# Output gate of the recurrence with features on partitions, and it and the first branch gate by seven products

## The chip, the cores and the metric

The kernel runs on one core of a Trainium2 chip. The metric is the device time of one execution in microseconds (us). The engines are named as in the profile: PE is TensorE, the matrix engine (PEld its loads of the stationary operand), DVE is VectorE, ACT is ScalarE, POOL is GpSimd and SP is SyncE, which here only starts DMA loads. Each of them works through its own queue in order, and a semaphore wait at the head of a queue holds up all that stands behind it.

## The reference, cut to what matters

Two layers of a decoder trunk over 512 tokens of width 1024, in float32. Each layer has a feed-forward block, a mixer and a second feed-forward block. The change is in the mixer:

```python
h = rms_norm(x, gn[2])
proj = h @ w_in[l]
hq, hf, hi, hg, aq, ak, av, gate_a, gate_b = jnp.split(proj, IN_SPLITS, axis=-1)
y_hg = hgrn2_mixer(hq, hf, hi, hg, lb_all[l], hgrn_head_gain[l]) @ w_branch_hgrn[l]
y_at = swa_sink_attention(aq, ak, av, attn_sinks[l]) @ w_branch_attn[l]
mixed = jax.nn.sigmoid(gate_a) * y_hg + jax.nn.sigmoid(gate_b) * y_at
x = x + rms_norm(mixed @ w_out[l], gn[3])
# the end of hgrn2_mixer: o [tokens, 4 heads, 128] is the output of the recurrence
o = o * rsqrt(mean(o * o, axis=-1) + EPS) * head_gain
o = o.reshape(B, S, 512) * silu(g_out)          # g_out is hg
```

`hq, hf, hi, hg` are 512 wide (four heads of 128), the two branch gates 1024.

## The kernel before, in words

**Products.** Every float32 product is made of rounded parts: an operand is split into a high part (`whi`, or `s`) and the low rest (`wlo`), and `mm3` issues three matmuls per 128x128 block of the stationary operand: high by high, high by low, low by high. `project` makes 128 features on partitions by 512 tokens (8 blocks deep, 24 matmuls of 512 columns); `project_tok` makes four tiles of 128 tokens on partitions by 512 features (96 matmuls of 512 columns). `sevenths` makes two such sets of 128 features at once by seven products over half of the tokens and half of the depth each, as in Strassen's scheme: 84 matmuls of 256 columns and one `lead` of 144 columns, where two `project` take 48 of 512. It needs sums of the weights' quarters (made on DVE while the weights stream in, lines 340 to 345, from two tiles `w32` into `tt`) and sums of the operand's quarters, kept in `x56` and `x37`, and on DVE five steps that put the products together in `m` (L1063 to L1070).

**The stream of weights.** `ws` loads weights by SP (L247) into four tiles `w32`, and prepares at most a few units ahead. A unit is split on ACT (L359, cast of the high part), and its low part is made either by a subtraction on DVE (L363) or, for the kind "v", by a negated copy on ACT (L355) and an accumulating DMA of POOL (L358).

**Order.** PE's order is written by hand: it is the order of the program. The small matmuls of attention and of the recurrence are placed between the large products by `Order`: each of these jobs is a coroutine that yields a waiting time from the table `WAIT`, and goes on when the products issued since then add up to it by a fixed rate per column. The queues of DVE and ACT are set by a scheduler, and their order is part of the built program.

**The mixer before.** `quad` makes q and forget gates of heads 0 and 1 of the recurrence; then come the projections of attention (`kS`, `qS`, `vT`), the values `vs` (`project_tok`), the output gate `gs` (`project_tok`, token tiles on partitions, tanh on ACT at L1428, two steps on DVE at L1429 and L1431, the second with the head gain `hgh`), and the projections of heads 2 and 3. `head` applies the sigmoids (L1272 to L1274 on ACT, L1275 to L1277 on DVE). `recurrence_scores` and `chunk_states` run the recurrence in levels (on DVE L1172, L1177, L1188, and predicated copies at L1164). `outputs` makes a head's output: the matmuls into `aux`, a square on ACT (L1289), the mean and its root (L1291 to L1293), the normed output (L1295), four products with `gs` (L1300), four transposes and a split. `attend` makes one block of attention: scores, bias (L1357), maxima (L1362), eight exponentials on ACT (L1374), their sums and shares on DVE (L1378 to L1382), transposes, copies on ACT (L1396), the values' product. Then follow the first branch, eight times `branch` (one `project` for the gate, 12 matmuls for the branch itself), with the operand sums `pre.sums()` ahead of the last four, and the second branch, four times `branches`, whose gates come by `sevenths`. `aux` and `acc` are the PSUM banks, `big` is a pool of 61 tiles of 128x512 (named `s` in the profile).

**The gain rows.** `hgh`, the head gain on every partition, is loaded among the constants at the start; `gain_rows` halves it on DVE and makes the lower bounds `lb`, `oml` behind that.

Of the kernel before, what the change touches and what calls it, by code (L numbers as in the profile page):

```python
# [7 lines left out]
F32 = mybir.dt.float32  # L8
F32R = mybir.dt.float32r
# [24 lines left out]
    head=2600.0, level=5000.0, last=3400.0, chunks=2600.0, states=2600.0, norm=2370.0, gate=8000.0,  # L34
    values=1200.0, scores=2000.0, exp=9000.0, shares=6000.0, turn=1900.0, turned=3000.0, rest=1200.0, lent=4200.0, apart=4000.0, block=2000.0, pair=4000.0, att0=1260.0, att1=12300.0,
)
W32, WS, AHEAD, TAIL, FIRST, EARLY, LATE = 4, 6, 3, 4, 7, 4, 8
# [9 lines left out]
def trunk(ctx: ExitStack, tc: tile.TileContext, xin, wall, gains, lbT, hgain, sinks, c_dist, c_mask, c_ident, out):  # L47
# [111 lines left out]
    class Stream:  # L159
# [29 lines left out]
        def gates(self):  # L189


            u, v, h = self.n, self.wall, (slice(0, D // 2), slice(D // 2, D))
            self.src[u + 1] = [(h[0], wall[v + 1][:, h[1]]), (h[1], wall[v + 2][:, h[0]])]
            self.src[u + 2] = [(h[0], wall[v + 1][:, h[0]]), (h[1], wall[v + 2][:, h[1]])]
            self.pairs(1)
            self.plain(1)
# [41 lines left out]
        def load(self, upto):  # L238
            while self.dma < min(upto, self.n):
                w = sb.tile([P, D], F32, tag="w32", name=nm("w32"), bufs=W32)  # L240
                u = self.dma
                if isinstance(self.src[u], list):
                    for c, a in self.src[u]:
                        nc.sync.dma_start(w.rearrange("p (m c) -> p m c", m=4) if c is None else w[:, c], a)  # L244
# [334 lines left out]
    class Pre(Quarters):  # L579


        def __init__(self, l, n):
# [5 lines left out]
            self.x56, self.x37 = [], []  # L588

        def sums(self):  # L590
# [6 lines left out]
            for x, v in zip((self.x56, self.x37), quarter_sums(a[0][0], a[1][0], a[0][1], a[1][1])):  # L597
                x.append(pair_split(v))

# [436 lines left out]
    def sevenths(pre, between=lambda: None, first=True):  # L1036
# [8 lines left out]
        p1, p26, p57, p43 = acc()[:, :H2], acc(), acc(), aux()  # L1045
# [220 lines left out]
    def mixer(l, pre, nxt):  # L1266
        vs, gs = [], []
# [12 lines left out]
        def outputs(i, h):  # L1280
# [15 lines left out]
            yield WAIT["norm"]  # L1296
            while len(gs) < TT:
                yield 500.0
            for t in range(TT):
                nc.vector.tensor_tensor(o[:, t, :], o[:, t, :], gs[t][:, i * P : (i + 1) * P], op=ALU.mult)  # L1300
            yield WAIT["gate"]
# [3 lines left out]
            oa[i] = split(pt)  # L1305
# [120 lines left out]
        for p in project_tok(pre):  # L1426
            g = big()
            nc.scalar.activation(out=g, in_=p, func=AF.Tanh, scale=0.5)  # L1428
            nc.vector.scalar_tensor_tensor(g, g, 1.0, p, op0=ALU.add, op1=ALU.mult)  # L1429
            gv = g.rearrange("p (i d) -> p i d", i=H)  # L1430
# [221 lines left out]
```

## Time and profile before

| | us |
|---|---|
| median of 3 runs (lowest, highest) | 2024.97 (2024.91, 2026.1) |
| the profiled execution | 2024.79 |
| its span in the trace | 2023.0 |
| PE busy | 2016.2 |
| DVE busy | 1624.3 |
| ACT busy | 1265.2 |
| POOL busy | 268.3 |

The mixer of layer 0 lies at about 338 to 650 us, that of layer 1 some 1000 us later. Rows of the timeline give start, duration, engine, line, operation, output and input, count, and in brackets the idle time before and what ended it. Rows of the chain give start, duration, engine, tile, line and count. Neighbouring steps of one engine overlap in the trace by a little, so what a step costs is read from start to start.

### The profile page before, as it was taken

How to read it: one execution, taken by the hardware profiler on the slowest of the kernel's cores; microseconds unless marked ns; L12 is line 12 of the kernel's file. 1: busy time of each engine (PE TensorE's matmuls, PEld its weight loads, DVE VectorE, ACT ScalarE, POOL GpSimd, SP SyncE). 2: the span in 40 equal slices, each digit the busy share in tenths (PEclk: the TensorE clock that was granted, in tenths of full speed). 3: DMA queues.
4: the chain of work that ended last, by engine and by line, in shares of the span. 5: the costliest groups of instructions: out<-in, count | busy, mean ns of one | idle time of the engine just before them, and what ended most of it. 6: DMA issues, size and time to landing. Idle time of an engine off the chain costs nothing.

```text
span 2023.0 us, 36425 instructions
## 1 busy us (share of the span) xinstructions
PE 2016.2 (100%) x13553; PEld 1809.1 (89%) x13553; DVE 1624.3 (80%) x2894; ACT 1265.2 (63%) x2213; POOL 268.3 (13%) x318
## 2 busy tenths in 40 slices
PE   9999999999999999999999999999999999999998
PEld 8899988877898999998899998898778989999987
DVE  5888899767786788888998888977686858888888
ACT  7566687447364566658766666864554646666684
POOL 0111140000000011113211111400000100111140
PEclk9999999999999999999999999999999999999999
DMA  8688798311246368879768888872122554788794
GB/s 257 159 193 198 177 203 244 109 63 64 83 104 208 112 158 190 193 189 208 202 170 196 196 190 203 189 223 86 61 74 63 151 182 123 170 193 200 175 202 122
DMA packets 166801, 328.07 MB, mean 162 GB/s; under 512 B 19072, under 2 KB 85088, under 8 KB 166624
## 3 DMA queue, kind: packets, MB, share of 16 engines
q1 hardware_dynamic: 122416, 228.16, 34.1%
q0 software_dynamic: 44064, 97.54, 28.5%
q8 instruction: 106, 1.74, 0.3%
q14 instruction: 71, 0.58, 0.1%
q10 hardware_dynamic: 144, 0.05, 0.0%
HBM read 213.43 MB, written 14.73 MB: 113 GB/s over the span
## 4 chain that ended last, share of the span: by engine, by line
PE 93%; DVE 3%; ACT 1%; DMA 1%; issue 1%; SPq 0%; DVEq 0%; ACTq 0%
PE acc L116 71%; PE aux L116 20%; PE aux L126 2%; DVE wlo L296 1%; DVE s L264 1%; DMA w<-wall 1%; PE acc L126 0%; ACT whi L288 0%; DVE s L968 0%; SPq L244 0%; ACT s L442 0%; ACT s L443 0%; DVE wlo L363 0%; DVE s L863 0%; DVE s L433 0%
## 5 line engine op out<-in xcount | busy, mean ns | idle before, releaser
L116 PE MATMUL acc<-s,whi 128*128 128x256 f32 (+1 forms) x4998 | 1018.9, 303 | 0.0
L116 PEld LDWEIGHTS acc<-s,whi 128*128 128x128 f32 x4998 | 791.5, 188 | 46.6 <-issue 3.2
L116 PE MATMUL acc<-s,wlo 128*128 128x256 f32 (+1 forms) x2488 | 752.5, 302 | 0.1
L116 PEld LDWEIGHTS acc<-s,wlo 128*128 128x128 f32 x2488 | 467.9, 188 | 23.3 <-DVE wlo L363 0.4
L116 PE MATMUL acc<-whi,s 128*128 128x512 f32 x1360 | 441.5, 393 | 0.0
L359 ACT CAST whi<-w 128x1024 fp32r<-128x1024 f32 (+1 forms) x310 | 286.1, 926 | 195.0 <-PE acc L116 124.5
L358 POOL DMA_DIRECT2D wlo<-w x178 | 154.6, 869 | 1200.2 <-ACT wlo L355 715.0
L116 PEld LDWEIGHTS acc<-whi,s 128*128 128x128 f32 x1360 | 255.3, 188 | 57.1 <-issue 3.2
L116 PE MATMUL acc<-wlo,s 128*128 128x512 f32 x680 | 265.5, 390 | 0.2 <-DVE wlo L296 0.2
L355 ACT ACTIVATE wlo<-w 128x1024 fp32r<-128x1024 f32 (+1 forms) x178 | 154.6, 869 | 137.1 <-PE aux L116 98.2
L116 PE MATMUL aux<-s,whi 128*128 128x256 f32 (+1 forms) x1296 | 226.9, 278 | 0.0
L359 ACT CAST whi<-tt 128x1024 fp32r<-128x1024 f32 x160 | 168.4, 1053 | 83.2 <-DVE tt L341 43.0
L363 DVE TENSOR_TENSOR wlo<-w,whi 128x1024 fp32r<-128x1024 f32 (+1 forms) x132 | 157.4, 1205 | 78.3 <-ACT whi L359 78.1
L363 DVE TENSOR_TENSOR wlo<-tt,whi 128x1024 fp32r<-128x1024 f32 x160 | 195.4, 1221 | 9.9 <-ACT whi L359 7.3
L116 PEld LDWEIGHTS aux<-s,whi 128*128 128x128 f32 x1296 | 195.8, 188 | 1.1 <-issue 0.5
L116 PE MATMUL aux<-s,wlo 128*128 128x256 f32 (+1 forms) x648 | 179.8, 277 | 0.0
L116 PEld LDWEIGHTS acc<-wlo,s 128*128 128x128 f32 x680 | 127.8, 188 | 27.0 <-DVE wlo L296 2.1
L116 PE MATMUL aux<-whi,s 128*128 128x512 f32 x432 | 143.7, 390 | 0.0
L444 POOL DMA_DIRECT2D s<-s x128 | 111.1, 967 | 223.5 <-ACT s L432 104.7
L116 PEld LDWEIGHTS aux<-s,wlo 128*128 128x128 f32 x648 | 121.6, 188 | 0.4
L296 DVE TENSOR_TENSOR wlo<-s,whi 128x512 fp32r<-128x512 f32 x160 | 102.7, 686 | 9.9 <-ACT whi L288 9.9
L1070 DVE TENSOR_TENSOR m<-aux,s 128x512 f32<-128x512 f32 x80 | 55.2, 690 | 52.0 <-PE aux L116 51.5
(184 smaller groups left out, 2485.1 us busy)
## 6 DMA issues: line engine op xcount, KB each, us to landing
w<-wall SPq DMA_DIRECT2D x267, 512.0 KB, 3.9
wlo<-w POOLq DMA_DIRECT2D x98, 512.0 KB, 5.4
w<-wall SPq DMA_DIRECT2D x224, 128.0 KB, 3.5
wlo<-w POOLq DMA_DIRECT2D x80, 256.0 KB, 4.2
s<-wall SPq DMA_DIRECT2D x128, 128.0 KB, 4.2
s<-s POOLq DMA_DIRECT2D x64, 256.0 KB, 4.6
x_d<-s SPq DMA_DIRECT2D x48, 256.0 KB, 4.7
s<-x_d SPq DMA_DIRECT2D x48, 256.0 KB, 5.1
```

What stands on the lines that cost most here:

```text
L116: nc.tensor.matmul(o, lhsT, rhs, start=start, stop=stop)
L126: nc.tensor.transpose(o, src, ident)
L264: pin(nc.vector.tensor_tensor(o[c], x[c], y[c], op=op))
L296: pin(nc.vector.tensor_tensor(it.lo[:, h[c]], w[c], it.hi[:, h[c]].bitcast(F32), op=ALU.subtract))
L355: i = nc.scalar.mul(it.lo[:, c], w[:, c], -1.0)
L358: nc.gpsimd.dma_start(it.lo[:, c].bitcast(F32), w[:, c], accum_op=ALU.add)
L359: i = nc.scalar.copy(it.hi[:, c], w[:, c])
L363: self.hold(nc.vector.tensor_tensor(it.lo[:, c], w[:, c], it.hi[:, c].bitcast(F32), op=ALU.subtract))
L444: nc.gpsimd.dma_start(lo.bitcast(F32), src, accum_op=ALU.add)
L1070: ws.hold(nc.vector.tensor_tensor(m[:, 1:3, :], pairs[2], v[:, ::-1, :], op=ALU.add))
```

## The change

The output gate `hg` is made with features on partitions, by two `sevenths`; tanh and product stand in `hg[i]`, and `outputs` transposes first and multiplies with the gain column `hcol` and `hg[i]` in one step on DVE that reads the transposes from PSUM. The eight plain gates of the first branch become four pairs by `sevenths`, with `acc` for its last bank. The operand sums are made earlier: `within` makes one of four after each of the four projections of heads 2 and 3, with the splits on ACT and by DMA of POOL, and `third` makes the operand of product 3 in place of the second half of `h` in the first gate product. Heads 2 and 3 are projected ahead of the gate. The gate's weights are loaded in four turned pieces each (`turned`), the branch's weights become kind "v". The head gain is loaded in `gain_rows`, into a tile of the pool, and brought on partitions by a product with the identity and a sum. New lines are 1 to 39 higher than old ones.

```diff
-W32, WS, AHEAD, TAIL, FIRST, EARLY, LATE = 4, 6, 3, 4, 7, 4, 8
+W32, WS, AHEAD, TAIL, FIRST, EARLY = 4, 6, 3, 4, 7, 4
+PLAIN = (False, False, False, False)
...
-        def gates(self):
+        def turned(self, v, n):
+
+            for m in range(0, n, 2):
+                for i in range(2):
+                    c = slice((m + i) * P, (m + i + 1) * P)
+                    self.src[self.n + i] = [
+                        (slice(2 * q * P, 2 * (q + 1) * P), wall[v + q].rearrange("p (i c) -> p i c", i=2)[:, :, c]) for q in range(KT // 2)
+                    ]
+                self.pairs(1)
+                self.wall -= 2
+
...
+        def sums(self):
+            for x, v in zip((self.x56, self.x37), self.quarters()):
                 x.append(pair_split(v))
+
+        def within(self):
+
+            s, t = self.quarters()
+            self.x56.append(pair_split(s, split_dma))
+            x = big(F32R, [P, 2, S // 2])
+            self.x7.append(split_dma(t[:, 1, :], to=(x[:, 0, :], x[:, 1, :])))
+            self.t3.append(t[:, 0, :])
+
+        def third(self):
+            while self.t3:
+                self.x3.append(split(self.t3.pop(0), to=cut(self.h[len(self.x3)], HALF[1])))
+
+        def operand(self, n):
+            if n in (3, 7) and self.x7:
+                return self.x3 if n == 3 else self.x7
+            return super().operand(n)
...
-    def sevenths(pre, between=lambda: None, first=True):
+    def sevenths(pre, between=lambda: None, first=True, get=aux):
...
-            yield WAIT["norm"]
-            while len(gs) < TT:
-                yield 500.0
-            for t in range(TT):
-                nc.vector.tensor_tensor(o[:, t, :], o[:, t, :], gs[t][:, i * P : (i + 1) * P], op=ALU.mult)
-            yield WAIT["gate"]
+            yield WAIT["outs"]
+            if hg[i] is None:
+                while hg[i] is None:
+                    yield 500.0
+                yield WAIT["norm"]
             pt = aux()
             for t in range(TT):
                 transpose(pt[:, t * P : (t + 1) * P], o[:, t, :])
-            oa[i] = split(pt)
+            g = hg[i]
+            nc.vector.scalar_tensor_tensor(g, pt, hcol[:, l, i % 2 : i % 2 + 1], g, op0=ALU.mult, op1=ALU.mult)
+            oa[i] = split(g)
...
-        for p in project_tok(pre):
-            g = big()
-            nc.scalar.activation(out=g, in_=p, func=AF.Tanh, scale=0.5)
-            nc.vector.scalar_tensor_tensor(g, g, 1.0, p, op0=ALU.add, op1=ALU.mult)
-            gv = g.rearrange("p (i d) -> p i d", i=H)
-            nc.vector.tensor_tensor(gv, gv, hgh[:, l : l + 1, :].to_broadcast([P, H, P]), op=ALU.mult)
-            gs.append(g)
-        order.spawn(run(2, [head(project(pre), project(pre), i) for i in range(2, H)]))
+        heads = []
+        for i in range(2, H):
+            pj = []
+            for _ in range(2):
+                pj.append(project(pre))
+                pre.within()
+            heads.append(head(*pj, i))
+        order.spawn(run(2, heads))
+
+        for i in range(0, H, 2):
+            v = sevenths(pre, lambda: pre.third(), get=acc)
+            for n in range(2):
+                g = big()
+                u = v[:, 2 * n : 2 * n + 2, :].rearrange("p i t -> p (i t)")
+                nc.scalar.activation(out=g, in_=u, func=AF.Tanh, scale=-0.5 if n else 0.5)
+                nc.vector.scalar_tensor_tensor(g, g, 1.0, u, op0=ALU.add, op1=ALU.mult)
+                hg[i + n] = g
...
-        def branches(get):
-
-            v = sevenths(pre)
+        def branches(get, bank=aux):
+
+            v = sevenths(pre, get=bank)
             src = get()
             for i in range(2):
...
-        for m in range(LATE):
-            if m >= LATE - 4:
-                pre.sums()
-            part.append(branch(attended))
-        part += [g for m in range(LATE, KT, 2) for g in branches(attended)]
+        for plain in PLAIN:
+            if plain:
+                part += [branch(attended) for _ in range(2)]
+            else:
+                part += list(branches(attended, acc))
...
-                ws.plain(2 * H + 2 + 8 + LATE * 3 // 2)
-                for _ in range(KT - LATE // 2):
+                ws.plain(10)
+                g = ws.wall
+                ws.wall += 4
+                ws.plain(4, "v")
+                ws.turned(g, H)
+                for plain in PLAIN:
+                    ws.gates(not plain)
+                for _ in range(KT // 2):
                     ws.gates()
                 ws.rows(KT, False)
...
-        pin(nc.vector.tensor_scalar(hgh, hgh, 0.5, None, op0=ALU.mult))
-
+        t = big(F32, [P, DEPTH, 2, P])
+        nc.sync.dma_start(t[:, :, 0, :], hgain.partition_broadcast(P))
+        for l in range(DEPTH):
+            nc.vector.tensor_tensor(t[:, l, 0, :], t[:, l, 0, :], ident, op=ALU.mult)
+            nc.vector.tensor_scalar(t[:, l, 1, :], t[:, l, 0, :], -0.5, None, op0=ALU.mult)
+            nc.vector.tensor_scalar(t[:, l, 0, :], t[:, l, 0, :], 0.5, None, op0=ALU.mult)
+            nc.vector.tensor_reduce(hcol[:, l, :], t[:, l, :, :], axis=AX.X, op=ALU.add)
```

SP near the start, the last weight loads of the first product group: rows of before (`hgh` was loaded eight rows ahead of these), then of the changed kernel. `w32` is a weight tile, `wall` all weights, `x_d` a tile in memory.

```order
L247 DMA w32_62_312<-wall 128x1024
L247 DMA w32_65_342<-wall 128x1024
L247 DMA w32_72_384<-wall 128x1024
L247 DMA w32_79_437<-wall 128x1024
L247 DMA w32_93_503<-wall 128x1024
L556 DMA x_d_79<-s_88_475 128x512
```

```order
L264 DMA w32_65_341<-wall 128x1024
L264 DMA w32_72_383<-wall 128x1024
L264 DMA w32_80_445<-wall 128x1024
L1591 DMA s_76_405<-hgain 128x2x128
L264 DMA w32_94_511<-wall 128x1024
L264 DMA w32_106_575<-wall 128x1024
```

The load of the head gain has moved behind the weight load `w32_79` (now `w32_80`); what reads it stands at the head of `gain_rows` on DVE, ahead of the lower bounds and of the first feed-forward gate.

ACT in the mixer of layer 0, from the square of head 0's output (L1289 before, L1327 now) on; `den` are the sums of the exponentials, `ss` the mean square. Before:

```order
L1289 ACTIVATE s_950_5263<-aux_949_5255 128x512
L1292 ACT_TABLE_LOAD
L1292 ACTIVATE ss_951_5265<-ss_951_5265,eps_t_83 128x4
L1369 ACT_TABLE_LOAD
L1369 ACTIVATE es_958_5300<-es_958_5300 128x8
L1396 COPY s_955_5287<-aux_953_5277 128x512
L1396 COPY s_956_5288<-aux_954_5278 128x512
L1374 ACTIVATE s_936_5187,den_959_5303<-s_936_5187,neg_957_5298 128x256 x2
L1374 ACTIVATE s_937_5191,den_959_5303<-s_937_5191,neg_957_5298 128x256 x2
L1374 ACTIVATE s_947_5241,den_959_5303<-s_947_5241,neg_957_5298 128x256 x2
L1374 ACTIVATE s_948_5245,den_959_5303<-s_948_5245,neg_957_5298 128x256 x2
L1289 ACTIVATE s_961_5320<-aux_960_5312 128x512
```

And now:

```order
L376 CAST whi_983_5427<-tt_954_5294 128x1024
L1408 ACT_TABLE_LOAD
L1408 ACTIVATE es_976_5374<-es_976_5374 128x8
L1413 ACTIVATE s_941_5227,den_977_5377<-s_941_5227,neg_975_5372 128x256 x2
L1413 ACTIVATE s_942_5231,den_977_5377<-s_942_5231,neg_975_5372 128x256 x2
L1413 ACTIVATE s_949_5275,den_977_5377<-s_949_5275,neg_975_5372 128x256
L459 CAST s_963_5325<-s_961_5319 128x512
L460 ACTIVATE s_964_5326<-s_961_5319 128x512
L459 CAST s_965_5330<-s_962_5320 128x256
L460 ACTIVATE s_965_5330<-s_962_5320 128x256
L1310 ACT_TABLE_LOAD
L1310 ACTIVATE s_966_5334<-acc_918_5109 128x512
```

Among the eight exponentials (of `s_941`, `s_942`, `s_949`, `s_950`; the last three follow in the next seven rows) now stand the split of an operand sum (`s_961`, `s_962`, lines 459 and 460) and the three sigmoids of head 2 (L1310 to L1312, with a table load before and after them). Ahead of the exponentials, behind the square, two casts of the gate's weight sums (L376) were added, the second of which heads these rows.

DVE at the same place, from the sum of that square (L1291 before, L1329 now) on. Before:

```order
L1291 TENSOR_REDUCE ss_951_5265<-s_950_5263 128x4
L1364 TENSOR_TENSOR mxs_933_5172<-mxs_933_5172,sink_130 128x8
L1366 TENSOR_SCALAR neg_957_5298<-mxs_933_5172 128x8
L1368 TENSOR_TENSOR es_958_5300<-sink_130,mxs_933_5172 128x8
L1293 RECIPROCAL ss_951_5265<-ss_951_5265 128x4
L1295 TENSOR_TENSOR s_952_5269<-aux_949_5255,ss_951_5265 128x512
L1378 TENSOR_TENSOR den_959_5303<-den_959_5303,es_958_5300 128x8
L1379 RECIPROCAL den_959_5303<-den_959_5303 128x8
L1382 TENSOR_TENSOR s_936_5187<-s_936_5187,den_959_5303 128x512
L1291 TENSOR_REDUCE ss_962_5322<-s_961_5320 128x4
L1407 TENSOR_TENSOR s_863_4786<-aux_967_5340,s_859_4782 128x128
L1407 TENSOR_TENSOR s_864_4787<-aux_967_5340,s_860_4783 128x128
```

And now:

```order
L1329 TENSOR_REDUCE ss_957_5309<-s_956_5307 128x4
L362 TENSOR_TENSOR tt_954_5294<-tt_954_5294,w32_880_4864 128x512
L380 TENSOR_TENSOR wlo_952_5290<-tt_953_5291,whi_951_5289 128x1024
L1403 TENSOR_TENSOR mxs_938_5212<-mxs_938_5212,sink_129 128x8
L1331 RECIPROCAL ss_957_5309<-ss_957_5309 128x4
L1405 TENSOR_SCALAR neg_975_5372<-mxs_938_5212 128x8
L1407 TENSOR_TENSOR es_976_5374<-sink_129,mxs_938_5212 128x8
L1333 TENSOR_TENSOR s_958_5313<-aux_955_5299,ss_957_5309 128x512
L613 TENSOR_TENSOR s_959_5315<-s_744_4041,s_745_4042 128x512
L613 TENSOR_TENSOR s_960_5317<-s_765_4116,s_766_4117 128x512
L380 TENSOR_TENSOR wlo_984_5428<-tt_954_5294,whi_983_5427 128x1024
L507 TENSOR_TENSOR s_961_5319<-s_960_5317,s_959_5315 128x256
```

Between the mean square and the normed output of head 0, and behind them, now stand the half sums (L362) and low parts (L380) of the gate's weights and the operand sums (L613, L507): the sums `den` of the exponentials, which followed the normed output at once, now come eleven instructions behind it.

More of the change, by code (lines that the diff above doesn't have):

```diff
@@ L33 @@
     first=0.0, spread=2300.0, squares=1700.0, lay=34500.0, laid=770.0, normed=7600.0, final=2600.0,
[L34 to L37 removed]
+    head=2600.0, level=5000.0, last=3400.0, chunks=2600.0, states=2600.0, norm=2370.0,
+    outs=8000.0, values=1200.0, scores=2000.0, exp=9000.0, shares=6000.0, turn=1900.0, turned=3000.0, rest=1200.0, lent=4200.0, apart=4000.0, block=2000.0, pair=4000.0, att0=1260.0, att1=12300.0,
+)
+W32, WS, AHEAD, TAIL, FIRST, EARLY = 4, 6, 3, 4, 7, 4
+PLAIN = (False, False, False, False)
 TURN = 0
@@ L1043, in product @@
                 wmm(o, ws.block(it, c + k), x[k], k == 0, k == 3)
[L1045 removed]
+        p1, p26, p57, p43 = acc()[:, :H2], acc(), acc(), get()
         s, v = big()[:, :H2], big(F32, [P, 2, H2])
```

20 lines of the change are left out of this document (13 added, 7 removed).

## The prediction

> **What bounds the kernel now.** I read the page first (busy shares, chain by engine), then the chain in order of time, then windows of 25 us, and last the rows of VectorE (DVE) and ScalarE (ACT) one by one inside the mixer.
>
> ```profile
> PE 2016.2 (100%) x13553; PEld 1809.1 (89%) x13553; DVE 1624.3 (80%) x2894; ACT 1265.2 (63%) x2213; POOL 268.3 (13%) x318
> PE 93%; DVE 3%; ACT 1%; DMA 1%; issue 1%; SPq 0%; DVEq 0%; ACTq 0%
> ...
> 98.07 6.80 PE acc L116 x60
> ...
> 941.28 43.52 PE acc L116 x192
> ...
> 425.00:450.00 25.00, 25.00 (x130) 19.64 (x130) 15.55 (x33) 11.38 (x32) 0.00 (x0) 1.00 0.27 85
> 450.00:475.00 25.00, 25.00 (x152) 19.29 (x151) 17.61 (x40) 16.50 (x36) 0.00 (x0) 1.00 0.13 43
> ...
> 454.00:498.00 44.00, 44.00 (x234) 33.64 (x233) 31.28 (x71) 31.48 (x73) 0.61 (x2) 1.00 0.20 65
> ```
>
> TensorE (PE) is busy for the whole span and carries 93% of the chain; what shortens its list of matmuls shortens the run, and what makes it wait lengthens it one for one. The two chain rows are runs without a gap and give the pitch: 43.52/192 = 0.2267 us for 512 columns, 6.80/60 = 0.1133 us for 256, exactly half. The windows (columns: PE, weight loads, DVE, ACT, POOL, granted clock) lie in the mixer of layer 0, where the change works. There PE is full, and DVE has work for 62 to 71% of the time. From 454 to 498 DVE does 71 instructions in 31.3 us, ACT 73 in 31.5: 13 us are free on each.
>
> **The change part by part.** *Products.* Per layer 288 matmuls of 512 columns go (96 of the output gate, 192 of the first branch) and six times seven products come: 504 of 256 columns and six leads of 144. Twice: 1008 x 0.1133 + 12 x 0.064 (144/512 of 0.2267) - 576 x 0.2267 = 114.2 + 0.8 - 130.6 = **-15.6 us**. It counts in full, as PE has no gap to lose it in. The Trainium skill ("TensorE: Matmul & The Clock Gate", section "Wait — 56ns, not 53.3ns?") gives a warm matmul N/2.4 GHz plus about 2.5 ns, 215.7 ns at 512 columns, which taxes many narrow matmuls and speaks against this change. By it an estimate is 576 x 0.2157 - 1008 x 0.1092 - 12 x 0.0625 = 13.4 us saved; the trace shows no fixed part (0.2267 is twice 0.1133), so the measurement decides.
>
> *What the other engines get.* The prices, from rows where a step is followed at once by the next:
>
> ```profile
> 468.01 1.07 DVE L1357 SCALAR_TENSOR_TENSOR s<-dist,aux 128x256 f32<-128x256 f32 x3
> 469.01 0.68 DVE L1362 TENSOR_REDUCE mxs<-s 128x2 f32<-128x512 f32 x1
> ...
> 476.50 1.29 DVE L1431 TENSOR_TENSOR s<-s,hgh 128x512 f32<-128x512 f32 x2
> 477.70 1.28 DVE L1429 SCALAR_TENSOR_TENSOR s<-s,acc 128x512 f32<-128x512 f32 x2
> ...
> 480.10 1.71 DVE L1300 TENSOR_TENSOR s<-s,s 128x128 f32<-128x128 f32 x8
> 481.72 0.17 DVE L1364 TENSOR_TENSOR mxs<-mxs,sink 128x8 f32<-128x8 f32 x1
> ...
> 493.12 2.35 DVE L363 TENSOR_TENSOR wlo<-w,whi 128x1024 fp32r<-128x1024 f32 x2
> ...
> 536.42 0.29 DVE L1164 COPY_PREDICATED s<-mask,aux 128x128 f32<-128x128 int32 x1
> ...
> 489.70 0.60 ACT L1272 ACTIVATE s<-acc 128x512 f32<-128x512 f32 x1
> 490.20 0.59 ACT L1273 ACTIVATE s<-acc 128x512 f32<-128x512 f32 x1
> 490.68 0.60 ACT L1274 ACTIVATE s<-acc 128x512 f32<-128x512 f32 x1
> 491.15 1.06 ACT L359 CAST whi<-w 128x1024 fp32r<-128x1024 f32 x1
> ```
>
> Start to start, DVE takes 0.60 us for 512 elements (476.50 to 477.70 for two), 0.33 for 256, 0.20 for 128, about 1.15 for 1024, 0.27 for a predicated copy and some 0.12 for the smallest; ACT 0.49 for 512 and 1.0 for 1024. By shape, DVE gets over the whole program +68 of 512, +19 of 256, -24 of 1024 and -26 of 128: 40.8 + 6.3 - 27.6 - 5.2 = +14 us, 0.7% of the span. ACT gets some +68 us (48 of 1024, 36 of 256, 24 of 512), POOL 64 more accumulating transfers, SP 40 more loads. Against 20%, 37% and 87% of idle time that is nothing on average, so I put no price on the loads, the lo parts that go from DVE to ACT and POOL, the gain column, and the gate read from the transposes' PSUM. The cover of these is the slack of the stages outside the stretch below; where it is gone, they stand in its sum.
>
> *The order.* What costs is that work piles up in one place. In before, heads 2 and 3 were projected after the gate and after heads 0 and 1 and attention were well on. Now their projections, the four operand sums between them and the weights' half sums for the gate stand on DVE and ACT together with attention and with the outputs of heads 0 and 1.
>
> ```profile
> 453.46 1.23 DVE L363 TENSOR_TENSOR wlo<-w,whi 128x1024 fp32r<-128x1024 f32 x1
> 454.64 0.69 DVE L1291 TENSOR_REDUCE ss<-s 128x4 f32<-128x512 f32 x1
> ...
> 462.67 0.17 DVE L1378 TENSOR_TENSOR den<-den,es 128x8 f32<-128x8 f32 x1 [5.44 <-ACT s L1374]
> ...
> 487.31 0.17 DVE L1378 TENSOR_TENSOR den<-den,es 128x8 f32<-128x8 f32 x1 [3.54 <-ACT s L1374]
> ...
> 449.84 0.91 PE aux L116 x12
> ...
> 455.30 0.87 PE aux L126 x8
> ...
> 454.00 0.60 ACT L1289 ACTIVATE s<-aux 128x512 f32<-128x512 f32 x1 [0.57 <-PE aux L116]
> 454.62 1.28 ACT L1292 ACT_TABLE_LOAD   x1
> ...
> 458.58 0.52 ACT L1374 ACTIVATE s<-s,neg 128x256 f32<-128x256 f32 x1
> 459.00 0.20 ACT L1374 ACTIVATION_READ_ACCUMULATOR s<-s,neg 128x1 f32 x1
> 459.09 0.51 ACT L1374 ACTIVATE s<-s,neg 128x256 f32<-128x256 f32 x1
> ...
> 462.54 0.58 ACT L1289 ACTIVATE s<-aux 128x512 f32<-128x512 f32 x1
> ```
>
> I take the stretch from the square of head 0's output (ACT, 454.0 in before) to the transposes in the second gate product that reuse a bank which DVE must first have read in the predicated copies of head 2's recurrence. In the new order PE has 320 matmuls and transposes between the two: 147 of 256 columns (16.7), 48 of 512 (10.9), 36 transposes (0.87/8 each, 3.9), 72 scores and shares (0.91/12 each, 5.5) and the recurrence's steps (an estimate of 6.5, at two to three times that each): 43.5 us. DVE has 144 instructions between the same two: 48 of 512 (28.8), 6 of 1024 (6.9), 49 of 256 (16.2), 9 predicated (2.4), 10 of 128 (2.0) and 22 small (2.6): **59 us**. The windows row agrees: 71 instructions took 31.3, so 144 take 63. DVE starts on them at about 455.3, since half sums stand ahead, and so ends at 514.5 at the earliest, where PE would want it at 497.5. That is **17 us per layer even if DVE never waits**.
>
> It does wait, for ACT. In before the eight exponentials were through 8.5 us after the square (454.0 to 462.5), and DVE idled 5.44 us for them. Now there stand among them two casts of half sums (2.1), the splits of an operand sum (1.6), a second pair of table loads (2.6) and the sigmoids of head 2 (1.5): 16.3 us, so the sums are ready near 470.3. DVE has some 9 us of work until then and idles 3 to 6. The same comes again with the sigmoids of head 3 (about 3 us) and the second eight exponentials (5). Walking both queues by hand, PE waits in steps that add up to about 10 us (for head 1's normed output), 20 (for the turned attention shares that ACT copies), 25, 28 and 33. The second level's wait is the one I trust least, as part of DVE's queue there may be ahead. Between 17 and 33 I take **28 us per layer, 56 in all**, nearer the upper end because the idle time is read from rows that exist. Later DVE is lighter by some 20 us per layer than before (28 more here, +7 over the layer), so nothing more is added.
>
> *The start.* The gain column is loaded later, behind a weight load on SP's queue.
>
> ```profile
> 41.08 2.73 PE acc L116 x12
> ...
> 35.39 0.28 DVE L1537 TENSOR_SCALAR hgh<-hgh 128x256 f32<-128x256 f32 x1
> 35.60 0.15 DVE L1540 TENSOR_TENSOR lbmx<-lb_in 128x4 f32<-128x4 f32 x1
> ...
> 38.69 0.68 DVE L1101 TENSOR_TENSOR s<-acc,s 128x512 f32<-128x512 f32 x1
> ...
> L247 SPq DMA_DIRECT2D w<-wall x1: 327/327/327, 38.8 to 38.8; - x1
> ...
> L1517 SPq DMA_DIRECT2D hgh<-hgain x1: 334/334/334, 15.6 to 15.6; - x1
> ...
> DMA to landing us min/median/max: 3.1/3.1/3.1
> ```
>
> The weight load just ahead of it was issued at 38.8, as it waits for a buffer. So the gain leaves at 39.1 and lands 3.1 later, 42.2; DVE wanted it at 35.4, and in its order stand behind it eight small steps (2.2), the lower-bound rows (35.60 to 38.69, some 2.5 with the table already loaded) and the first gate's step, which frees the bank of the products at 41.08: freed at 47.5, **+6.5 us once**. Bounds: 0 if SP comes by earlier, 9 if ACT's exponential adds its table load.
>
> The profiled execution took 2024.79, which is 1.8 more than its span and 0.2 below the median of the runs, so both count as the same: 2024.8 - 15.6 + 56 + 6.5 = **2072 us**.
>
> **The rivals.** *DVE's throughput alone* (waits for ACT lie under queued work): 17 per layer, 2024.8 - 15.6 + 34 + 6.5 = 2050, or 2043 without the start. For it: the 13 us that DVE and ACT have free per 44, which show that queues slide; against it: DVE idled 5.44 and 3.54 us for exponentials even with half the work.
>
> *Faster: the pile does not bind.* If DVE gets through the stretch in PE's 43.5 us, the products decide: 2024.8 - 15.6 = 2009, or 2016 with the start. It decides at 43.5/144 = 0.30 us per instruction. For it: DVE is at 80% and PE never waits now. Against it: the same stretch runs at 0.44 each, and 48 of the 144 cost 0.60.
>
> *The clock falls too.* The forecast has PE wait up to 10 us at a time.
>
> ```profile
> 2000.00:2010.00 10.00, 9.50 (x46) 7.50 (x45) 6.03 (x13) 2.58 (x6) 0.00 (x0) 1.00 0.37 105
> 2010.00:2020.00 10.00, 8.25 (x51) 6.80 (x49) 6.95 (x12) 3.37 (x9) 0.00 (x0) 1.00 0.21 61
> ```
>
> Here PE idles 1.75 us of 10 and the clock stays at 1.00; no row shows a longer wait. If after each of some nine waits PE ran at half clock for 3.4 us, 1.7 would be lost each, at most 15: 2087. Most of it would lie where PE waits for DVE next anyway. The Trainium skill (same page, section "What's actually happening") has the clock drop to half after an idle window of about 3.4 us and come back after as long; no run here shows it yet.
>
> *The gate and the loads cancel*: stalls of 8 per layer would give no change; no row speaks for that size.
>
> **How the numbers follow.** Forecast (2058 to 2084, the walk with 22 to 33 per layer) 0.60; throughput alone 0.22; clock 0.08; the pile does not bind 0.08; cancelled 0.02. A change below 0.2% (4 us) can't be told from none in this kernel. Only the fourth is faster, the last is the same, and the rest slower: 0.08, 0.02, 0.90. The range goes from throughput alone without the start, 2043, to the clock rival with 30 per layer, 2090, and leaves out 0.1 to 0.15.
>
> **What would show it.** Right: in both mixers (here 455 to 530) PE has gaps that sum to 20 to 30 us, ended by DVE (by the new line numbers: normed output L1333, level steps L1226, predicated copies L1202) and by ACT (turned shares L1435), while DVE runs at over 80% in these windows; a gap of 6 to 7 us near 41, ended by DVE; later pairs of the first branch run without a gap at the pace of seven products. Wrong: PE full in 455 to 530 means that DVE's steps were not needed where I put them or cost less; gaps named by weight loads or lo parts mean that the new turned loads are late; a clock under 1.00 after gaps favours the clock rival; no gap near 41 means that SP's queue was ahead.

## The result and the profile after

The changed kernel takes **2093.0 us** (median, 2090.6 to 2094.0) against 2025.5 (2024.9 to 2026.2): ratio 1.0332, 95% interval 1.0319 to 1.0346. It is slower, as forecast, but 21 us more than forecast and 3 us above the range. The traced execution took 2090.6, the lowest of the four. Its page, in the rows that answer to those of before (span, busy time, chain by engine):

```profile
span 2088.8 us, 37805 instructions
PE 2022.3 (97%) x13997; PEld 1832.5 (88%) x13997; DVE 1642.2 (79%) x2933; ACT 1337.2 (64%) x2321; POOL 324.3 (16%) x382
PE 84%; DVE 8%; ACT 4%; DMA 2%; issue 2%; SPq 0%; DVEq 0%; ACTq 0%; POOLq 0%
```

PE is now idle for 66.5 us of the span (6.8 before) and DVE and ACT have entered the chain. What PE waited for (total, times, longest):

```profile
PE aux L117 <- ACT s L1435: 14.8, 2, 7.4
PE aux L127 <- DVE s L1202: 8.6, 2, 4.3
PE acc L117 <- DVE s L1139: 8.2, 1, 8.2
PE aux L127 <- ACT s L1435: 7.6, 2, 3.8
PE acc L117 <- DMA s<-s: 7.5, 2, 3.7
PE aux L117 <- DVE mv L1226: 7.2, 2, 3.6
PE aux L117 <- DVE s L1333: 2.4, 2, 1.2
PE aux L117 <- DVE s L1202: 2.0, 2, 1.0
```

One wait is at the start; all others come twice, once per mixer, at the lines that the prediction named, and one that it did not (the accumulating DMA of the operand sums). They make 25 us per mixer. The chain's two long runs without a gap, of the attention projections ahead of the mixer's critical part and of the feed-forward block behind it, measure a mixer, before and after:

```profile
352.37 23.11 PE acc L116 x160
...
697.03 32.07 PE acc L116 x230
```

```profile
363.24 23.11 PE acc L117 x160
...
734.34 32.07 PE acc L117 x230
```

The first mixer went from 344.7 to 371.1 us, and all ahead of it is 10.9 us later. The second went from 344.6 to 371.5. So 10.9 + 26.4 + 26.9 = 64.2 of the 65.8 us between the spans lie in the three places that were forecast.

The start (SP, landing, DVE, PE):

```profile
L1591 SPq DMA_DIRECT2D s<-hgain x1: 1327/1327/1327, 39.8 to 39.8; - x1
...
DMA to landing us min/median/max: 5.7/5.7/5.7
...
45.51 0.49 DVE L1593 TENSOR_TENSOR s<-s,ident 128x128 f32<-128x128 f32 x2 [8.90 <-DMA s<-hgain]
...
50.20 1.19 PE L117 MATMUL acc<-s,whi 128*128 128x512 f32 x2 [8.24 <-DVE s L1139]
```

The mechanism is the forecast one; the load left at 39.8 (forecast 39.1), but needed 5.7 us to land where `hgh` had needed 3.1. Its own issue took longer too, 1.33 us against 0.33.

In the mixer, ACT's square of head 0's output and the end of the eight exponentials (the next square follows them at once), the windows of the stretch, and four windows inside it (PE, weight loads, DVE, ACT, POOL, granted clock, DMA share, GB/s):

```profile
464.18 0.60 ACT L1327 ACTIVATE s<-aux 128x512 f32<-128x512 f32 x1 [4.51 <-PE aux L117]
...
480.88 0.58 ACT L1327 ACTIVATE s<-aux 128x512 f32<-128x512 f32 x1
...
454.00:545.00 91.00, 65.76 (x473) 53.97 (x472) 73.46 (x179) 58.04 (x125) 11.93 (x15) 0.87 0.32 70
...
475.00:477.50 2.50, 0.00 (x0) 0.00 (x0) 1.33 (x3) 2.47 (x5) 0.66 (x1) 0.83 0.92 147
477.50:480.00 2.50, 0.45 (x2) 0.29 (x4) 0.34 (x1) 2.49 (x6) 0.00 (x0) 0.50 0.08 10
480.00:482.50 2.50, 2.50 (x8) 0.47 (x4) 1.42 (x4) 2.49 (x7) 0.23 (x1) 0.50 0.00 0
482.50:485.00 2.50, 2.50 (x9) 1.55 (x8) 2.47 (x6) 2.48 (x7) 0.64 (x1) 0.81 0.58 102
```

The exponentials are through 16.7 us after the square (8.5 before, 16.3 forecast). DVE is busy for 81% of 454 to 545 and ACT for 64%: neither is full, and PE waits for whichever is late. PE stood still from 472 on; from about 476.7 it is granted half its clock, and it stays at half until about 483.5.

### The profile page after: what moved, and what is told of

It is laid out like the page before. It is cut to its first block, busy times and chain, and to the rows that moved or that the text cites. A ratio compares the mean times of both kernels' runs of the same rounds, so it can differ in the third digit from the quotient of the medians.

```text
span 2088.8 us, 37805 instructions
## 1 busy us (share of the span) xinstructions
PE 2022.3 (97%) x13997; PEld 1832.5 (88%) x13997; DVE 1642.2 (79%) x2933; ACT 1337.2 (64%) x2321; POOL 324.3 (16%) x382
## 3 DMA queue, kind: packets, MB, share of 16 engines
q1 hardware_dynamic: 132400, 228.16, 33.5%
## 4 chain that ended last, share of the span: by engine, by line
PE 84%; DVE 8%; ACT 4%; DMA 2%; issue 2%; SPq 0%; DVEq 0%; ACTq 0%; POOLq 0%
PE acc L117 64%; PE aux L117 19%; PE aux L127 1%; DVE wlo L313 1%; DMA w<-wall 1%; DVE wlo L380 1%; DVE s L281 1%; DVE s L1006 1%; ACT s L1413 1%; ACT s L459 1%; DVE s L450 1%; ACT whi L305 0%; PE acc L127 0%; ACT s L460 0%; DMA s<-xin 0%
## 5 line engine op out<-in xcount | busy, mean ns | idle before, releaser
L117 PE MATMUL acc<-s,whi 128*128 128x256 f32 (+1 forms) x5426 | 1070.4, 298 | 16.5 <-DVE s L1139 8.2
L117 PEld LDWEIGHTS acc<-s,whi 128*128 128x128 f32 x5426 | 854.3, 189 | 61.1 <-issue 17.2
L117 PE MATMUL acc<-s,wlo 128*128 128x256 f32 (+1 forms) x2696 | 799.5, 297 | 0.1
L117 PEld LDWEIGHTS acc<-s,wlo 128*128 128x128 f32 x2696 | 510.6, 189 | 18.5 <-DVE wlo L380 0.4
L375 POOL DMA_DIRECT2D wlo<-w x226 | 196.4, 869 | 1400.0 <-ACT wlo L372 833.8
L117 PE MATMUL acc<-whi,s 128*128 128x512 f32 x1232 | 395.6, 391 | 0.0
L376 ACT CAST whi<-w 128x1024 fp32r<-128x1024 f32 (+1 forms) x310 | 280.5, 910 | 145.7 <-PE acc L117 69.6
L372 ACT ACTIVATE wlo<-w 128x1024 fp32r<-128x1024 f32 (+1 forms) x226 | 199.9, 886 | 139.5 <-PE aux L117 97.3
L376 ACT CAST whi<-tt 128x1024 fp32r<-128x1024 f32 x184 | 193.8, 1053 | 120.3 <-DVE tt L358 67.2
L380 DVE TENSOR_TENSOR wlo<-tt,whi 128x1024 fp32r<-128x1024 f32 x184 | 224.8, 1222 | 15.1 <-ACT whi L376 12.3
L380 DVE TENSOR_TENSOR wlo<-w,whi 128x1024 fp32r<-128x1024 f32 (+1 forms) x84 | 99.0, 1196 | 47.5 <-ACT whi L376 44.5
L459 ACT CAST s<-s 128x256 fp32r<-128x256 f32 (+1 forms) x144 | 73.0, 507 | 48.1 <-DVE s L510 19.5
```

What stands on the lines that cost most here:

```text
L117: nc.tensor.matmul(o, lhsT, rhs, start=start, stop=stop)
L372: i = nc.scalar.mul(it.lo[:, c], w[:, c], -1.0)
L375: nc.gpsimd.dma_start(it.lo[:, c].bitcast(F32), w[:, c], accum_op=ALU.add)
L376: i = nc.scalar.copy(it.hi[:, c], w[:, c])
L380: self.hold(nc.vector.tensor_tensor(it.lo[:, c], w[:, c], it.hi[:, c].bitcast(F32), op=ALU.subtract))
L459: nc.scalar.copy(hi, src)
```

## The experiments

Four questions: is the start the gain's load; does the half clock cost time of its own; what makes the pile (the work of DVE and ACT that piles up in the mixer); and is the products' gain there at all. Times are medians; the kernel before took 2024.7 to 2025.0 on the same chips.

**The start.** The gain is loaded among the constants again.

```diff
+    hgh = const([P, DEPTH, P], "hgh")
+    nc.sync.dma_start(hgh, hgain.partition_broadcast(P))
...
-        nc.sync.dma_start(t[:, :, 0, :], hgain.partition_broadcast(P))
-            nc.vector.tensor_tensor(t[:, l, 0, :], t[:, l, 0, :], ident, op=ALU.mult)
+            nc.vector.tensor_tensor(t[:, l, 0, :], hgh[:, l, :], ident, op=ALU.mult)
```

> The changed kernel, but with the head gain loaded among the constants at the start, as before the change; the gain column is still made from it. Theory: the gap of 8.2 us near 42 us and about 2 us of half clock behind it are this load alone, so 2093 - 10 = 2083 us. Rival: the bank would be late anyway (the column's eight steps on DVE, the exponential on ACT), and 2 to 3 us come back: 2090.

Measured 2082.4 (ratio 1.0283, 1.0268 to 1.0298): 10.6 us less. The theory holds. All kernels below but the two fills, the first with a later recurrence and the last have this edit.

**The clock.** Idle matmuls keep PE busy while it waits.

```diff
+    def idle(o, n):
+        for _ in range(n):
+            nc.tensor.matmul(o[:, :P], ones, ones, start=True, stop=True)
...
             po = aux()
+            idle(po, 30 if n == 1 else 0)
...
+                idle(pe[0], {(2, 1): 16, (3, 0): 16}.get((n, b), 0))
...
+        idle(p57, fill)
         product(p57[:, :H2], w, 0, 5)
```

> The changed kernel with idle matmuls of ones put into PE's queue ahead of five waits of each mixer (30, 14, 16, 14 and 16 of 128 columns, some 0.22 us each), into banks that are free there, so that PE stays busy while it would wait. They make nothing that is used. Theory: the half clock after the gaps costs time of its own, about 8 us per layer, so 2093 - 16 = 2077 us with a clock of 1.00 in the mixers. Rival: the clock's loss lies where PE waits for DVE or ACT next anyway, so the time stays at 2093 (within 3).

Measured 2097.6 (1.0359, 1.0343 to 1.0374). The first fill missed its place: its bank `po` comes free by the very copy that PE waits for, so it stood behind the wait and added to it:

```profile
480.12 9.25 PE L128 MATMUL aux<-ones 128*128 128x128 f32 x60 [7.37 <-ACT s L1443]
```

This run tells nothing on the question. The next gives that fill a bank of its own (`idle(acc(), 30)`).

> As the kernel with filled waits, but the first fill (30 idle matmuls) goes into a bank of its own, since in that run it stood behind the wait that it was to fill and so added 9.3 us per layer; the second fill is 18 instead of 14. Theory: the half clock costs time of its own; PE's busy time was 21.7 us above the sum of its matmuls, some 3 of it at the start, so 2093 - 18 = 2075 us. Rival (absorbed in the next waits): 2090 to 2095.

Measured 2086.4 (1.0305, 1.0288 to 1.0322): 6.6 us less, between the two, nearer the rival. In both mixers the clock stays at 1.00. Yet PE meets DVE and ACT at the same time as before the fill. Two waits of the changed kernel, and the same two with fills, whose mixer's first run begins at 364.13 instead of 363.24:

```profile
508.00 1.11 PE L127 MATMUL aux<-ident,s 128*128 128x128 f32 x4 [3.82 <-ACT s L1435]
...
516.61 0.39 PE L117 MATMUL aux<-mv,s 128*64 128x96 f32 x4 [3.60 <-DVE mv L1226]
```

```profile
364.13 23.11 PE acc L117 x160
...
508.85 0.66 PE L131 MATMUL aux<-ident,s 128*128 128x128 f32 x4 [1.24 <-ACT s L1443]
...
517.45 0.39 PE L117 MATMUL aux<-mv,s 128*64 128x96 f32 x4 [1.82 <-DVE mv L1231]
...
733.01 32.07 PE acc L117 x230
```

PE goes on 145 and 153 us after the start of that run in both. What PE gains at full clock it waits away at the next meeting; only what follows the last wait of a mixer is gained, some 2 us of each. This run also measures the pile without the clock's loss, since its fills and waits can be added up:

```profile
L128 PE MATMUL acc<-ones 128*128 128x128 f32 x192 | 22.1, 275 | 0.0
L128 PE MATMUL aux<-ones 128*128 128x128 f32 x184 | 21.5, 275 | 0.0
```

21.8 us of fills per mixer, and 8.8 and 8.1 us in which PE is still idle: 30.2 on average. The lengths of the mixers, 368.9 and 369.7 us, say the same: they are 30.4 above the 338.9 us for which PE is busy in a mixer of e14 below, which has all of the change's matmuls at the full clock.

**What makes the pile: the recurrence of heads 2 and 3.** It is begun 30 us later in the hand-written order; the gain's load is not moved here.

```diff
-        order.spawn(run(2, heads))
+        order.spawn(run(2, heads), 30000.0)
```

> The changed kernel with the recurrence of heads 2 and 3 begun 30 us later in the hand-written order. Theory (the pile on DVE and ACT costs by the order in which PE meets it): the waits for the level steps and predicated copies (3.6 + 1.0 + 4.3 us per layer) and the clock behind them go, about 11 us per layer: 2071 us. Rival (DVE lacks throughput over the whole mixer): the same work is met later, 2088 to 2095.

Measured 2069.1 (1.0216, 1.0199 to 1.0233): 24 us less, as by the theory (22). The waits for level steps and predicated copies are gone, the others stay:

```profile
PE aux L117 <- ACT s L1435: 14.7, 2, 7.4
PE aux L127 <- ACT s L1435: 7.6, 2, 3.8
PE acc L117 <- DMA s<-s: 7.5, 2, 3.7
```

**The hand-off through ACT and DMA, or DVE's throughput?** The operand sums are split on DVE.

```diff
-            self.x56.append(pair_split(s, split_dma))
+            self.x56.append(pair_split(s))
...
-            self.x7.append(split_dma(t[:, 1, :], to=(x[:, 0, :], x[:, 1, :])))
+            self.x7.append(split(t[:, 1, :], to=(x[:, 0, :], x[:, 1, :])))
```

> With the gain early; the operand sums are split by a cast on ACT and a subtraction on DVE, instead of two copies on ACT and an accumulating DMA of POOL. Theory (PE waits on hand-offs through ACT and the DMA): the wait for the DMA (3.7 per layer) goes and ACT's copies come 2 to 4 us earlier: 2082 - 14 = 2068 us. Rival (DVE's throughput): DVE gets 3.8 us more per layer in the pile, 2088 to 2092.

Measured 2085.3 (1.0296, 1.0281 to 1.0312), against 2082.4 with the split as it was. The wait for the DMA is gone, and another grew by more (3.8 before):

```profile
PE aux L127 <- ACT s L1435: 8.8, 1, 8.8
PE aux L117 <- ACT s L1435: 7.0, 1, 7.0
```

The theory's time (2068) falls: with the wait at the DMA gone, PE waits for ACT's copies instead. What the hand-off costs by itself the run does not say, since the same edit gives DVE 3.8 us more per layer. The rival's size (2088 or more) was not reached either.

**Later attention.** `turned=10500` and `turn=5800` instead of 3000 and 1900 in `WAIT`, and the recurrence 30 us later.

> With the gain early, the recurrence of heads 2 and 3 begun 30 us later, and in each attention block the shares' transposes 3.9 us and their product 7.5 us later in the hand-written order. Theory: the waits for ACT's copies (7.4 + 3.8 per layer) and the half clock behind them go too; left are the DMA (3.7) and 1.2: 2069 - 10 - 30 = 2029 us. Rival (the work has no room anywhere): the first branch waits for attention instead, 2050 to 2060.

Measured 2095.5 (1.0348, 1.0332 to 1.0363), a clear miss: without the two waiting times these edits should give some 2058 (the gain early and the recurrence later, 10.6 + 24 less). PE's waits in the first mixer:

```profile
PE aux L117 <- ACT s L1435: 8.5, 1, 8.5
PE aux L117 <- DVE mv L1226: 5.9, 2, 3.9
PE acc L117 <- ACT s L459: 4.3, 1, 4.3
PE acc L117 <- DMA s<-s: 3.5, 1, 3.5
PE aux L127 <- DVE s L1343: 3.5, 1, 3.5
```

The waits moved to other places, and in both mixers together they grew; which meeting makes each of them was not worked out. Placing attention later is no cure.

**The operand sums left out.** `within` is not called, and products 3, 5, 6 and 7 read raw halves.

```diff
-                pre.within()
...
-            if n in (3, 7) and self.x7:
-                return self.x3 if n == 3 else self.x7
+            if self.n == 2 and n in (3, 5, 6, 7):
+                return self.raw(n % 2, 0)
```

> The changed kernel with the gain early, in its order, but without the operand sums: products 3, 5, 6 and 7 of the mixer read raw halves of h, so that some 12 us of DVE and 7.5 us of ACT per layer are left out and all matmuls stay. Theory (DVE and ACT have too much to do between the head's output and the second gate product): each mixer loses 12 to 15 us of waiting, 2082 - 27 = 2055 us. Rival (the order of table loads, sigmoids and exponentials on ACT sets the waits, whatever DVE has): under 10 in all, 2073 or more.

Without the sums these products, here and in the next three runs, are not those of the layer; the matmuls are the same. Measured 2050.0 (1.0122, 1.0108 to 1.0136): 32.4 us less, more than the DVE work of 24 that was left out. The theory holds, the rival falls. ACT's splits (19 us by the busy times) and the sums' accumulating DMAs went with them, so the run does not say which engine's share weighs most.

> As the kernel without operand sums, and the recurrence of heads 2 and 3 begun 30 us later. Theory (the pile is a sum of parts): the waits for level steps and predicated copies (16 us in that run's two mixers, and 2 of clock) go: 2050 - 18 = 2032 us. Rival: DVE's work is met later all the same, 2043 or more.

Measured 2028.1 (1.0017, 1.0007 to 1.0026): 22 less again, nearly the 24 that the same edit gave with the sums in. The parts add up.

**The place of heads 2 and 3.** As e12, and their projections and weights behind the gate:

```diff
-                ws.plain(4, "v")
                 ws.turned(g, H)
+                ws.plain(4, "v")
```

(and the two loops of the mixer exchanged).

> As the kernel without operand sums, but heads 2 and 3 are projected behind the gate again, as before the change. Theory (the new place of heads 2 and 3 makes the other half of the pile): 20 us of waiting per mixer shrink to under 5: 2015 to 2022 us. Rival (the weights' half sums of the gate's products, or head 0's and 1's outputs, make it): 2040 to 2050.

Measured 2021.7 (0.9985, 0.9976 to 0.9995), inside the theory's range: 28.4 us below e12. PE's busy time, and what it still waits for in the mixers:

```profile
PE 2005.7 (99%) x13997; PEld 1823.8 (90%) x13997; DVE 1616.3 (80%) x2877; ACT 1310.7 (65%) x2277; POOL 309.5 (15%) x366
...
PE aux L127 <- DVE s L1396: 2.8, 2, 1.4
PE aux L117 <- ACT mv L1224: 2.3, 4, 0.8
PE aux L117 <- DVE s L1396: 1.7, 4, 0.6
```

With sums and order both taken away, PE is busy for 10.5 us less than before the change (2016.2): this is what the products gain, where 15.6 was forecast. In the two mixers alone it is 5.6 and 5.7.

**The weights' half sums.** As e13, the gate's products on raw weights.

```diff
+            if it.kind == "b" and getattr(it, "bare", False):
+                self.t13, self.t = w, v
```

> As the kernel without operand sums and with the recurrence later, and the gate's products use raw weights instead of their half sums (9 us less of DVE per layer). All matmuls of the change stay. Theory: PE hardly waits any more and what is left is the products' own gain, less the 4 us that the run without seven products lost: 2024.8 - 15.6 + 4 = 2013 us. Rival (seven products are slower by themselves than their columns say): 2020 or more with PE busy all the time.

Measured 2028.5 (1.0020, 1.0010 to 1.0030), no different from e13 (2028.1), so the half sums cost nothing there, where the pile is gone; what they cost in the whole change was not run. PE waited as in e13 (12.7 us in the mixers against 13.4), so the theory's 2013 was a miss, and the rival's condition (PE always busy) wasn't met: the run doesn't test it.

**The change in parts, all computed.** First without any new product: the gate on partitions by four plain projections (`turned` with plain units, `hcol` for all four heads), heads 2 and 3 behind it, the branch's weights and the operand sums as before the change, `PLAIN = (True,) * 4`.

> The change without its products: all first branch gates plain, operand sums where they were, heads 2 and 3 behind the gate; left are the gate and its product with features on partitions, one step on DVE from PSUM behind the transposes, and the gain column, loaded early. Theory: this part is hidden, 2024 to 2027 us. Rival: it costs by itself (transposes wait for the gate, one more reader of a bank): 2030 or more.

Measured 2028.8 (1.0020, 1.0011 to 1.0029), 4 us more than before: a small miss. PE never waits in the mixers, and is busy for 3.8 us more with the same number of matmuls: 1.4 in each mixer and 1.3 ahead of the first. Attention's scores and its product with the values, in the first mixer of before and of this run:

```profile
L116 PE MATMUL aux<-s,s 128*64 128x512 f32 x28 | 6.9, 607 | 0.0
L116 PE MATMUL aux<-s,s 64*128 64x256 f32 x72 | 6.4, 295 | 0.0
```

```profile
L117 PE MATMUL aux<-s,s 128*64 128x512 f32 x28 | 7.5, 609 | 0.0
L117 PE MATMUL aux<-s,s 64*128 64x256 f32 x72 | 7.4, 297 | 0.0
```

The two are busy for 1.6 us more per mixer; their instructions take as long, but follow each other more slowly. Why is open; a wait that the trace does not name would look so.

Then with seven products in one pair (`PLAIN = (True, True, True, False)`, `within` ahead of branches 2 to 5), and in two pairs (`within` ahead of branches 0 to 3), that also with the split on DVE, and with the recurrence 15 us later:

> Gain early, the gate on partitions by four plain projections, heads 2 and 3 behind it; the operand sums stand ahead of plain branches 2 to 5, when the recurrence of heads 2 and 3 is nearly through, and only the last pair of the first branch goes by seven products. Theory (seven products gain where no pile is): 2024.8 - 2 x 1.3 = 2022.2 us. Rival: the sums still meet the recurrence, 2028 to 2032.

> Seven products with the order of before: gain loaded early, gate on partitions by four plain projections, heads 2 and 3 behind it, operand sums made ahead of the first four plain branches, and only the last two pairs of the first branch by seven products. Theory: PE never waits, and two pairs per layer save 48 x 0.2267 - 84 x 0.1133 - 0.06 = 1.3 us each: 2025.5 - 5.2 = 2020 us. Rival: the seven products themselves bring the waits (sums of weights, loads in pieces): 2025 or more.

> Products in place with the operand sums split on ACT and DVE alone. In the run before, PE waited 4.2 us in the first mixer for the recurrence's copies on ACT, which stood behind these splits. Theory: these waits go, 2036.6 - 2 x (4.2 + 1.7) = 2025 us. Rival: DVE is late instead, 2035.

> Products in place (two pairs of the first branch by seven products) with the recurrence of heads 2 and 3 begun 15 us later. Theory: its waits of 4.2 us and the half clock of 1.7 in each mixer were the meeting of operand sums and recurrence, and go: 2036.6 - 12 = 2025 us or a little less. Rival: the meeting is only moved to the weights' sums of the seven products, 2034 to 2040.

Measured 2028.4 (1.0017, 1.0008 to 1.0026), 2036.6 (1.0056, 1.0041 to 1.0071), 2038.8 (1.0068, 1.0053 to 1.0083) and 2043.9 (1.0097, 1.0083 to 1.0110): all four are misses.

With one pair (e9) the rival has the time, but not the cause: PE never waits in the mixers, and each takes 345.1 us against 346.1 in e11. So the seven products do gain where no pile is, 1.0 us where 1.3 was forecast (the medians differ by 0.4 in all); the theory missed because the kernel that it builds on, e11, is itself 4 us slower than before. With two pairs PE does wait: for the recurrence's copies, which on ACT stand behind splits of the operand sums and low parts of the weights (first mixer of e4, the two pairs):

```profile
PE aux L117 <- ACT mv L1227: 2.3, 1, 2.3
PE aux L117 <- DVE mv L1229: 1.4, 1, 1.4
```

The rivals of these three have the direction, and that of e4 its time. Those of e8 (2035) and e10 (2034 to 2040) are too low: the split on DVE did not help, and a later recurrence made it worse.

Last the kernel before, with its own gate and order, and only the last pair by seven products (`LATE = 6`):

> The kernel before, with its token-tiled gate, its order and its gain, and only the last pair of the first branch by seven products; the operand sums are the changed kernel's (split on ACT and by DMA, product 3's operand in place of the second half of h), made ahead of plain branches 2 to 5. Theory: the mixers of the last-pair run took 1.05 us less each than those of the run without seven products, and the old gate saves the 1.5 us per mixer that the gate on partitions cost there: 2024.8 - 2.1 = 2022.7 us. Rival: no difference that can be told, 2024 to 2026.

Measured 2040.4 (1.0078, 1.0065 to 1.0092), a miss as well. One copy of ACT in the chunk states holds PE in each mixer, and ACT itself stood idle ahead of it, for a DMA (row of the first mixer; the accumulating transfers of an operand sum were issued at 558.0):

```profile
PE aux L116 <- ACT s L1280: 12.2, 2, 6.4
...
563.08 0.27 ACT L1280 COPY s<-aux 128x128 f32<-128x128 f32 x1 [4.48 <-DMA s<-s]
```

The copy takes a tile of the pool, so one that these transfers still held is the likely reason; no run tests it.

None of these kernels that computes the whole layer beats the one before.

## Why the prediction was right or wrong

The sign, the three places and the mechanism held; three terms of the sum were off, all to the same side.

| term | forecast | measured | from |
|---|---|---|---|
| products | -15.6 | -10.5 | PE's busy time, e14 against before |
| start | +6.5 | +10.6 | e1 |
| pile in two mixers | +56 | +65 to +68 | lengths of the mixers; what is left of 2093.0 - 2024.8 |
| sum | +47 | +68 | |

*The pile: the step that failed is the choice of 28 within 17 to 33*, with the clock at nothing. These are the mixers of layer 0 by the traces:

| kernel | length | PE busy |
|---|---|---|
| before | 344.7 | 344.6 |
| changed | 371.1 | 345.9, part of it at half clock |
| changed, with fills (e5) | 368.9 | 360.1, of which 21.8 are fills |
| e14 | 342.3 | 339.0 |

Both mixers of the changed kernel are on average 32.4 us longer than PE's 338.9 of e14. Of these, 2.0 are the clock's (the fills of e5 took them back), and 30.4 are waits of the pile, against 28. The walk of both queues gave 33 per mixer, and I took off 5 because I did not trust one of its waits. As a time of meeting the walk was right: from the square of head 0's output to the transposes at the end of the stretch it had 43.5 + 33 = 76.5 us, and the traces have 76.9 (464.2 to 541.1) and 77.3, without the clock's loss 76.1 (e5). The loss is 30.4 and not 33 because PE's own work there is 45.5 us (67.3 busy in e5, less 21.8 of fills) and not 43.5: the trace has 384 matmuls there where 320 were counted. (Within that count the 6.5 us for the recurrence do not follow either: 17 matmuls are left for it, at two to three times 0.076 us 2.6 to 3.9.) Wait by wait the walk was wrong: head 1's normed output, which it gave the first 10 us, held PE for 1.2, and the shares, the DMA and later steps for the rest. In this change the end of the stretch was surer than its waits. The reason given, that idle times were read from rows, spoke for 33 and not for 28.

*Which parts make it* was right: operand sums 32.4 us (e12), place of heads 2 and 3 28.4 (e14), together 61 of the 68; PE still idles for 6.8 in the mixers of e14. The rival of throughput alone (17 per mixer) falls: DVE is idle for a fifth of the stretch, and the loss is nearly twice as large. Whether the half sums add to the pile, as I counted, is open: they cost nothing where it is gone (e15).

*The start:* place and order were right; the load left 0.7 us later than forecast, the landing took 5.7 instead of 3.1, and half a clock for 3.2 us behind the gap was left out of the sum.

*The clock rival:* the clock does fall, 4.5 us after PE stopped at 472.2, and half of it is granted from 476.7 to 483.5. The Trainium skill's rule ("TensorE: Matmul & The Clock Gate", section "What's actually happening") fits: it names an idle window of about 3.4 us, and the half clock here lasts twice that. That most of it lies where PE waits next anyway was right: PE is busy for 7 us more in a mixer than in e14, and the fills took back 2 of them (6.6 in the whole run by the medians). But "most" was priced at nothing.

*The products:* pitch and count were right (three matmuls of 256 columns take 0.34 us in e14 too), yet a mixer gains 5.7 us of the 7.8. Of the missing 2.1, 1.2 are small matmuls: in e14 attention's product with the values takes 7.4 us instead of 6.4, as in e11, and the recurrence's 0.2 more. The six `lead` cost some 0.12 each instead of 0.064 (579.51 to 579.86 in e14 for one and two matmuls of 256 columns). The rest is open, and so is 0.8 us outside the mixers. I had costed the gate on partitions at nothing; by e11 it costs 1.4 us in each mixer. The Trainium skill's fixed part per matmul (same page, section "Wait — 56ns, not 53.3ns?") would have given 13.4, nearer to what came, but for another reason: the pitch shows no such part.

*Faster, or PE full* was rightly given little.

## What to carry to other kernels

Fewer matmuls pay only where the vector engines can feed them. Count the instructions of each engine between two meetings with PE, before and after, at prices from the trace, and walk the queues in order. Here DVE's sum alone gave about half of the loss, though DVE was at 80% on average; the waits for ACT between its steps made the rest. Do not discount such a walk because one of its waits looks doubtful: here the waits came elsewhere, and the end of the stretch came within a microsecond of the walk. And give a price to what "mostly" hides under another wait: the clock, priced at nothing, cost 4 to 7 us here.

## What the runs showed of the hardware

Half a clock costs little when the next wait is set by another engine: with fills PE reached two meetings at the same time (145 and 153 us into the mixer) as with the clock down. The load of the head gain took 3.1 us to land when issued among the constants and 5.7 us when issued between two weight loads. It is not quite the same transfer: its rows there go to two places of a tile, and the page of the profile counts 128 more packets than in e1 (132400 against 132272), so how much is due to the place is open. The same small matmuls of attention ran 9 to 16% slower (6.9 to 7.5 us, 6.4 to 7.4 us per mixer) in e11, which changes what stands around them and not them. In e14 only the second kind is slower, in e13 neither; why is open.
